# Seven block products for eight: a two-layer encoder trunk with Strassen's scheme in its large products

## The chip, the cores and the metric

One core of a Trainium2 chip runs the whole program. The metric is the device time of one execution in microseconds (us), as the median of several executions; lower is better. The core has TensorE (PE in the profile, its weight loads PEld), VectorE (DVE), ScalarE (ACT), GpSimd (POOL) and SyncE (SP, which issues all DMAs here). TensorE writes to PSUM, 8 banks of 128 partitions x 2 KB; everything else lies in SBUF.

## What is computed

x is 1024 tokens x 1024 features, float32. Layer A is multi-scale retention, layer B latent attention; both add to the residual stream.

```python
h = rmsnorm(x, g_pre)
proj = h @ w_in                           # q, k: 8 heads x 128; v, gate: 8 heads x 256
q, k, v, gate = jnp.split(proj, [...], axis=-1)
q = rope(q); k = rope(k) * 128 ** -0.5
# chunks of 64: inner scores, and a state R carried over chunks with a decay per head
o = groupnorm(inner + cross)
h1 = x + rmsnorm((jax.nn.silu(gate) * o) @ w_out, g_post)
# layer B
c_kv, k_r = split(rmsnorm(h1, g_kv) @ w_kv_a, [256])     # 256 + 64 columns
c_q, gate = split(rmsnorm(h1, g_pre) @ w_in_b, [384])    # 384 + 1024 columns
# queries, keys and values from the normalised latents, chunk-causal softmax attention, 8 heads
out = h1 + rmsnorm((jax.nn.silu(gate) * o) @ w_out_b, g_post)
```

The change touches four products: x with `w_in` (1024 x 1024 x 6144), the output product of layer A (1024 x 2048 x 1024), the latents (1024 x 1024 x 704) and layer B's gates (1024 x 1024 x 1024).

## The kernel before

A float32 operand of a large product is held as hi + lo, both of a rounded float32 type (fp32r): hi is the rounded value and lo the exact rest. `mm3` (lines 75 to 80) makes a product of three passes, lo x hi, hi x lo, hi x hi, into one PSUM bank. `split` (L84, L85) writes hi on ACT and lo on DVE; `split_scaled` (L89, L90) does the same with a factor for each partition.

**Memory.** `Heap` holds 51 blocks of 4 KB in every partition and hands them out in the order in which they were freed. A new tile in a block waits until the last reader of the old one is done.

**Order of the work.** The code is written in one order; the framework's planner then places each engine's instructions at build time, by that order among those that its own model holds to be ready. So passes of neighbouring k tiles can change places, and ready work can move into a gap. On the chip each engine keeps the order so fixed. `later(n, fn)` and `tick` write the mixing of a head n units of products behind its projections. `inv_rms` (L98 to L103: DVE, then a power on POOL) is emitted at high priority. All DMAs are issued by SP.

**Weights.** `weight_order` lists all weights in the order of use. `fetch` (L152) loads one of 128 x 1024, `prefetch` splits it, and two or three further ones are under way.

**Layer A** runs once for each half of 512 tokens. `load_x` brings x transposed, scales it by the gains and splits it (L254, L255). The products take this x before its normalisation; 1 / rms of the rows is computed on the side (`load_rows`, `ropeq_for`) and enters with the rotation tables (`csq`), the scale of v, and the gates (`rsb`, L369). `ret_pair` makes two heads: q and k with features on partitions (`features`, eight k tiles of three passes, 512 wide), then `rotate` on DVE (L312 to L315); v with tokens on partitions, 512 columns for both heads; the gates. `ret_scores`, `ret_states` and `ret_mix` mix the tokens, in blocks of 128. `ret_out` multiplies with `w_out_a` in two column halves, four PSUM banks each, eight heads deep; since both halves of the tokens run through all this, all weights of layer A are loaded and split twice. After the second half, `post_a` and `norm_transpose` build hT, the normalised and transposed input of layer B, split.

**Layer B.** `latents` makes c_kv with the rotary key (320 columns) and c_q (384 columns) for eight token tiles, in two groups of four, straight from PSUM into the norms. `gates` makes eight heads of gates, two halves each. The last four token tiles of layer A are normalised while the first group's latents run. `attention` follows, and is not touched by the change.

Of the kernel before, what the change touches and what calls it, by code (L numbers as in the profile page):

```python
# [10 lines left out]
F32 = mybir.dt.float32  # L11
# [14 lines left out]
NH = 8  # L26
# [3 lines left out]
LAG = 2  # L30


class Heap:
    """4 KB blocks of every partition, reused in the order in which they were freed."""
# [17 lines left out]

class Trunk:
# [12 lines left out]
    # ---------------------------------------------------------------- helpers  # L66
# [8 lines left out]
    def mm3(self, ps, lhs, rhs, first, last):  # L75
        """ps += lhs^T rhs with lhs = (hi, lo), rhs = (hi, lo)."""
        mm = self.nc.tensor.matmul
        mm(ps, lhs[1], rhs[0], start=first, stop=False)  # L78
        mm(ps, lhs[0], rhs[1], start=False, stop=False)  # L79
        mm(ps, lhs[0], rhs[0], start=False, stop=last)  # L80

    def split(self, hi, lo, src):
        """hi + lo = src."""
        self.nc.scalar.activation(hi, src, AF.Copy)  # L84
        self.nc.vector.tensor_sub(lo, src, hi.bitcast(F32))  # L85

    def split_scaled(self, hi, lo, src, scale):
        """hi + lo = src * scale, scale one number per partition."""
# [4 lines left out]
    def inv_rms(self, ss, n, tag, width):  # L93
        """(ss / n + eps) ** -0.5 for the columns of ss."""
# [3 lines left out]
    def _inv_rms(self, ss, n, tag, width):  # L98
        nc = self.nc
        r = self.small([P, width], tag, bufs=2)  # L100
        nc.vector.tensor_scalar(out=r, in0=ss, scalar1=1.0 / n, scalar2=EPS, op0=ALU.mult, op1=ALU.add)
# [6 lines left out]
    def tick(self):  # L108
        """One unit of a product is emitted: what has waited long enough follows it."""
# [7 lines left out]
    # ---------------------------------------------------------------- weights  # L117
    def weight_order(self):
        """All weights in the order of their use: (source, columns, gains)."""
        I, G = self.I, self.gains  # L120
        for half in range(2):
            for p in range(NH // 2):
                for j in range(12):
                    yield I["w_in_a"][p, j], (1024,), None
            for n in range(2):
                for k in range(NH):
                    yield I["w_out_a"][n, k], (1024,), None
# [918 lines left out]
```

## Time and profile before

| | |
|---|---|
| median of 3 runs | 1349.33 us (1348.61 to 1349.94) |
| profiled execution: its span | 1346.5 us, 2.8 us below the median of the runs |
| PE busy | 1329.0 us, 6952 matmuls |
| DVE, ACT, POOL busy | 829.2, 562.4, 72.1 us |
| DMA | 120.19 MB, 89 GB/s in the mean |
| mean granted TensorE clock | 0.999 |

The profile gives no other time of the profiled execution than its span; the 2.8 us are the difference to the other runs. "Busy" counts an engine from the start to the end of its instructions, where those of PE overlap. The chain of waits is followed back from the last instruction: at each step it goes to what released the instruction, or to the one before it on its engine. A row of a group has its line, engine, operation, output and inputs, count, then busy time and the mean of one instruction in ns, then the idle time of the engine ahead of it.

### The profile page before, as it was taken

The numbers are of one execution on the slowest core, as the hardware profiler recorded it, in microseconds if no ns is written. First come the engines' busy times: TensorE is split into PE (matmuls) and PEld (weight loads), VectorE is DVE, ScalarE is ACT, GpSimd is POOL, SyncE is SP. The second block draws the span as 40 slices with busy tenths as digits, with TensorE's granted clock in tenths as the row PEclk, the third lists the DMA queues.
The fourth block names the chain that finished last, engine by engine and source line by source line (L and its number), as shares of the span: only waits on it lengthen the run. The fifth ranks groups of instructions, "written<-read, shape, count | busy, mean of one in ns | idle before, by whom it ended". The sixth has DMA issues, their size and how long they took to land.

```text
span 1346.5 us, 17839 instructions
## 1 busy us (share of the span) xinstructions
PE 1329.0 (99%) x6952; PEld 1141.9 (85%) x6952; DVE 829.2 (62%) x1576; ACT 562.4 (42%) x998; POOL 72.1 (5%) x112
## 2 busy tenths in 40 slices
PE   7999999999999999999999999999999999999997
PEld 6888888888888888888888889988888989898886
DVE  4865666655747575656755865440089888888632
ACT  5533333335624333333435826431154545456311
POOL 0001000000001000000000102100000000000000
PEclk9999999999999999999999999999999999999999
DMA  9222232225445322232234351120011010122231
GB/s 357 87 79 73 63 99 74 79 83 182 132 156 182 95 78 63 63 110 78 64 110 122 116 177 63 48 73 30 24 32 42 25 42 25 42 73 79 88 116 47
DMA packets 38804, 120.19 MB, mean 89 GB/s; under 512 B 5184, under 2 KB 5440, under 8 KB 38720
## 3 DMA queue, kind: packets, MB, share of 16 engines
q1 hardware_dynamic: 38720, 119.06, 27.5%
q8 instruction: 54, 0.88, 0.3%
q14 instruction: 30, 0.25, 0.1%
HBM read 106.46 MB, written 8.39 MB: 85 GB/s over the span
## 4 chain that ended last, share of the span: by engine, by line
PE 94%; DVE 2%; ACT 1%; DMA 1%; issue 1%; SPq 1%; POOL 0%; DVEq 0%; POOLq 0%; ACTq 0%
PE acc L79 24%; PE acc L78 24%; PE acc L80 24%; PE r L78 4%; PE r L80 4%; PE r L79 4%; PE r L884 2%; PE S L838 1%; PE r L389 1%; PE r L478 1%; PE S L842 1%; PE S L839 1%; PE S L840 1%; PE S L843 1%; SPq L759 1%
## 5 line engine op out<-in xcount | busy, mean ns | idle before, releaser
L85 DVE TENSOR_TENSOR wlo<-wraw,whi 128x1024 fp32r<-128x1024 f32 (+4 forms) x165 | 192.4, 1173 | 141.1 <-ACT whi L84 123.6
L84 ACT ACTIVATE whi<-wraw 128x1024 fp32r<-128x1024 f32 (+4 forms) x165 | 167.6, 1022 | 169.6 <-PE acc L80 49.1
L78 PE MATMUL acc<-xhi,wlo 128*128 128x512 f32 x512 | 202.0, 395 | 6.5 <-ACT xhi L89 6.5
L79 PE MATMUL acc<-xlo,whi 128*128 128x512 f32 x512 | 200.8, 392 | 0.3 <-DVE xlo L90 0.3
L80 PE MATMUL acc<-xhi,whi 128*128 128x512 f32 x512 | 200.4, 391 | 0.0
L78 PEld LDWEIGHTS acc<-xhi,wlo 128*128 128x128 f32 x512 | 96.8, 189 | 25.3 <-ACT xhi L89 6.8
L80 PEld LDWEIGHTS acc<-xhi,whi 128*128 128x128 f32 x512 | 96.7, 189 | 20.2
L79 PEld LDWEIGHTS acc<-xlo,whi 128*128 128x128 f32 x512 | 96.8, 189 | 19.6 <-DVE xlo L90 1.3
L78 PE MATMUL acc<-whi,xlo 128*128 128x512 f32 x248 | 97.2, 392 | 0.0
L79 PE MATMUL acc<-wlo,xhi 128*128 128x512 f32 x248 | 96.6, 390 | 0.0
L80 PE MATMUL acc<-whi,xhi 128*128 128x512 f32 x248 | 96.4, 389 | 0.0
L854 ACT ACTIVATE p<-S,nm 128x896 f32<-128x896 f32 (+3 forms) x64 | 47.4, 741 | 54.9 <-DVE nm L851 50.2
L84 ACT ACTIVATE pT<-r 128x512 fp32r<-128x512 f32 (+2 forms) x96 | 44.5, 488 | 37.4 <-PE r L884 37.2
L460 ACT ACTIVATE y<-r,nb,rg 128x256 f32<-128x256 f32 x64 | 32.7, 562 | 54.5 <-DVE nb L457 54.5
L80 PEld LDWEIGHTS acc<-whi,xhi 128*128 128x128 f32 x248 | 46.6, 188 | 9.8
L78 PEld LDWEIGHTS acc<-whi,xlo 128*128 128x128 f32 x248 | 46.6, 188 | 9.3
L79 PEld LDWEIGHTS acc<-wlo,xhi 128*128 128x128 f32 x248 | 46.6, 188 | 9.1
L85 DVE TENSOR_TENSOR pT<-r,pT 128x512 fp32r<-128x512 f32 (+2 forms) x96 | 50.9, 549 | 4.9 <-ACT pT L84 4.5
L369 DVE TENSOR_TENSOR sg<-acc,rsb 128x512 f32<-128x512 f32 x32 | 22.1, 690 | 50.0 <-PE acc L80 50.0
L78 PE MATMUL acc<-whi,ylo 128*128 128x512 f32 x128 | 50.7, 396 | 0.0
L78 PE MATMUL acc<-whi,u 128*128 128x512 f32 x128 | 50.0, 391 | 0.0
L80 PE MATMUL acc<-whi,yhi 128*128 128x512 f32 x128 | 49.9, 390 | 0.0
(245 smaller groups left out, 3152.4 us busy)
## 6 DMA issues: line engine op xcount, KB each, us to landing
wraw<-in_w_in_a_dram SPq DMA_DIRECT2D x94, 512.0 KB, 3.7
wraw<-in_w_out_a_dram SPq DMA_DIRECT2D x32, 512.0 KB, 3.7
xr<-in_xT_dram SPq DMA_DIRECT2D x16, 256.0 KB, 4.2
xt<-in_x_dram SPq DMA_DIRECT2D x8, 512.0 KB, 6.0
xres<-in_x_dram SPq DMA_DIRECT2D x8, 512.0 KB, 4.5
h<-xres SPq DMA_DIRECT2D x8, 512.0 KB, 2.9
wraw<-in_w_gate_dram SPq DMA_DIRECT2D x8, 512.0 KB, 3.4
rr<-ra SPq DMA_DIRECT2D x64, 64.0 KB, 2.0
```

Source lines behind the costliest of these rows:

```text
L78: mm(ps, lhs[1], rhs[0], start=first, stop=False)
L79: mm(ps, lhs[0], rhs[1], start=False, stop=False)
L80: mm(ps, lhs[0], rhs[0], start=False, stop=last)
L84: self.nc.scalar.activation(hi, src, AF.Copy)
L85: self.nc.vector.tensor_sub(lo, src, hi.bitcast(F32))
L369: nc.vector.tensor_mul(c, ps, self.rsb[:, :HALF])
L389: nc.tensor.matmul(pa[:, c], k32[:, c], q32[:, c], start=True, stop=True)
L460: nc.scalar.activation(y[:, i * 256:(i + 1) * 256], po[:, i, :], AF.Identity, bias=nb[:, i:i + 1], scale=rg[:, i:i + 1])
L478: nc.tensor.transpose(pt[:, n * P:(n + 1) * P], y[:, n * 256 + e * P:n * 256 + (e + 1) * P], self.ident)
L759: nc.sync.dma_start(r[64 * part + 32 * x:64 * part + 32 * x + 32, :], a[64 * x + 32 * i:64 * x + 32 * i + 32, :])
L854: nc.scalar.activation(p[:, :w].rearrange("p (a b) -> p a b", a=pieces), view, AF.Exp, bias=nm, accum_out=sm)
L884: nc.tensor.transpose(pt[:, k, :], p[:, (k0 + k) * P:(k0 + k + 1) * P], self.ident)
```

## The change

The four products are cut into 2 x 2 blocks each and made by seven block products in place of eight, in Winograd's form of Strassen's scheme. With A the activations and B the weights: S1 = A21 + A22, S2 = S1 - A11, S3 = A11 - A21, S4 = A12 - S2, and T1 = B12 - B11, T2 = B22 - T1, T3 = B22 - B12, T4 = B21 - T2. A11 x B11 gives a, which is copied out of PSUM into U (ACT); S2 x T2 is added to U, and so on (DVE); A12 x B21, A22 x T4 and S4 x B22 go on accumulating in banks that already hold a, S3 x T3 and S1 x T1.

- **Layer A's input.** Both token halves together. x is normalised before its split (`scale_x`: squares on ACT, column sums with a matrix of ones on PE, `inv_rms`, a broadcast by PE, eight scalings on DVE). The seven left operands, 28 blocks, stay in SBUF for all 24 weight pairs. Until the second half of x is there, the first three pairs do the two products that need only the first half (`EARLY`).
- **Weights.** `Units` loads a weight pair once (two blocks), makes its four T sums on POOL (`make_sums`) and splits seven units of 128 x 512 columns, up to three ahead.
- **v** comes out with features on partitions like all others; `ret_values` transposes it back on PE (16 transposes of 128 x 128 a head). Rotation (`rotate_a`) takes its swapped halves by two ACT copies and works on both q and k at once on DVE. The scale of v and the factor of the gates are gone.
- **y** of each head and half goes to DRAM; `out_a` reads it back and works by 28 steps of 24 matmuls. Its S sums are on DVE, its T sums on POOL.
- **Layer B's operands** are built from both token halves in `post_a`. `latents` takes 704 columns as 2 x 352, weights scaled by their gains on POOL, results kept in SBUF (`lat`) ahead of the norms. `gates` uses `Units` and `pair`; six finished gates go to DRAM and come back.
- The unit order, heap and attention code stay. The DMA scratch is set to 1024 bytes.

The core of the diff:

```diff
+class Units:
+    def fetch(self):
...
+        for j in range(2):
+            r = self.raw[p][j]
+            T.nc.sync.dma_start(r, src[j])
...
+    def make_sums(self, p):
+        sub = T.nc.gpsimd.tensor_sub
+        sub(ta[:, lo], r0[:, hi], r0[:, lo])
+        sub(tb[:, lo], r1[:, hi], ta[:, lo])
+        sub(ta[:, hi], r1[:, hi], r0[:, hi])
+        sub(tb[:, hi], r1[:, lo], tb[:, lo])
...
+    def prep(self):
+        u = T.heap.get("unit", F32R)
+        T.split(u[:, :HALF], u[:, HALF:], src)
...
+WINOGRAD = ("B11", "T2", "T3", "T1", "B21", "T4", "B22")
+    def product(self, ps, units, name, more=False):
+        u = units.next()
+        for k in range(4):
+            c, x = slice(k * P, (k + 1) * P), slice((k % 2) * HALF, (k % 2 + 1) * HALF)
+            self.mm3(ps, (u[:, :HALF][:, c], u[:, HALF:][:, c]), [b[:, x] for b in self.X[name][k // 2]],
+                     not more and k == 0, k == 3, more)
...
+    def pair(self, units, sink, steps="abcdefg", st=None):
+            if s == "a":
+                st["a"] = self.bank("acc")
+                self.product(st["a"], units, "A11")
+                st["u"] = self.small([P, HALF], "u2", bufs=4)
+                self.nc.scalar.copy(st["u"], st["a"])
+            elif s == "b":
+                b = self.bank("acc")
+                self.product(b, units, "S2")
+                add(st["u"], b, st["u"])
+            elif s == "c":
+                self.product(st["c"], units, "S3")
+                add(st["u3"], st["c"], st["u"])
+            elif s == "d":
+                self.product(st["d"], units, "S1")
+                sink(1, 1, st["d"], st["u3"])
+            elif s == "e":
+                self.product(st["a"], units, "A12", more=True)
+                sink(0, 0, st["a"], None)
+            elif s == "f":
+                self.product(st["c"], units, "A22", more=True)
+                sink(1, 0, st["c"], st["u"])
+            elif s == "g":
+                self.product(st["d"], units, "S4", more=True)
+                sink(0, 1, st["d"], st["u"])
...
     def layer_a(self):
+        x = self.load_x(0)
+        units.fetch()
+        self.scale_x(x)
+        A["A11"], A["A12"] = x[:2], x[2:]
+        self.left_sums(A, ("A11", "A12"))
...
+        x = self.load_x(1)
+        for sink, st in early:
+            self.pair(units, sink, "ae", st)
+        self.scale_x(x)
+        A["A21"], A["A22"] = x[:2], x[2:]
+        self.left_sums(A, ("A22", "S1", "S2", "S3", "S4"))
+        for sink, st in early:
+            self.pair(units, sink, "bcdfg", st)
+        for p in range(EARLY, 3 * NH):
+            self.pair(units, make(p))
...
+    def out_a(self):
+            if prod == 6:
+                return [left(1, 0, b), left(1, 1, b), left(0, 0, b)], [right(0, 0, b), right(0, 1, b), right(1, 1, b)]
...
+        run(1, X)
+        run(2, X, True)
+        run(6, Y)
+        run(7, X)
+        run(5, Y)
+        run(4, X, True)
+        for t in range(HT):
+            add(y[HT + t][:, n0], X[t], U[t])
+            self.post_a(HT + t, y[HT + t], gpost)
+        run(3, Y, True)
+        self.left_sums(self.A, ("A22",))
+        self.left_sums_keep(self.A)
+        for t in range(HT):
+            add(y[t][:, n1], Y[t], U[t])
+            self.post_a(t, y[t], gpost)
...
     def latents(self):
+        run(X, "S1", "T1")
+        run(X, "A22", "T4")
+        self.left_sums(self.A, ("A11", "A12", "S2", "S3", "S4"))
+        run(X, "A11", "B11")
+        run(Y, "S2", "T2")
+        run(X, "A12", "B21", True)
+        run(X, "S3", "T3")
+        self.latent_tiles(1, lat[HT:], rk)
+        run(X, "S4", "B22")
+        self.latent_tiles(0, lat[:HT], rk)
...
     def gates(self):
+        for p in range(NH // 2):
+            self.pair(units, sink(p))
+        for h in range(away):
+            self.gT[h] = heap.get("gT")
+            nc.sync.dma_start(self.gT[h], self.gd[h])
```

More of the change, by code (lines that the diff above doesn't have):

```diff
@@ L30 @@
 LAG = 2
+LAT = 704
+LH = LAT // 2
 class Heap:
@@ L188, in run @@
         self.h1 = dp.tile([NT, P, DM], F32, name="h1")
+        self.yd = [[dp.tile([P, DM], F32, name=f"yd{h}_{half}") for half in range(2)] for h in range(NH)]
+        self.gd = [dp.tile([P, DM], F32, name=f"gd{h}") for h in range(NH)]
         self.ident = self.small([P, P], "ident")
```

910 lines of the change are left out of this document (536 added, 374 removed).

## The prediction

> **What bounds the kernel now.** I read the engine totals first, then the chain that ended last, then what TensorE waited for, then the stages.
>
> ```profile
> PE 1329.0 (99%) x6952; PEld 1141.9 (85%) x6952; DVE 829.2 (62%) x1576; ACT 562.4 (42%) x998; POOL 72.1 (5%) x112
> ...
> PE 94%; DVE 2%; ACT 1%; DMA 1%; issue 1%; SPq 1%; POOL 0%; DVEq 0%; POOLq 0%; ACTq 0%
> ```
>
> TensorE (PE) is busy for 1329.0 of 1346.5 us and makes up 94% of the chain. The view of TensorE's waits:
>
> ```profile
> PE acc L78 <- ACT xhi L89: 6.5, 1, 6.5
> PE r L564 <- DVE hT L85: 1.2, 1, 1.2
> ```
>
> Its only long wait is the start. So the time is the number of matmuls times their spacing, plus some 17 us of gaps. By stage (columns: stretch, its length, busy time of PE, PEld, DVE, ACT, POOL, granted clock, DMA share, GB/s):
>
> ```profile
> 0.00:30.00 30.00, 23.23 (x91) 18.24 (x92) 14.62 (x20) 19.04 (x27) 1.72 (x7) 1.00 0.93 353
> ...
> 45.00:345.00 300.00, 300.00 (x1517) 253.73 (x1516) 190.58 (x324) 116.88 (x170) 21.10 (x32) 1.00 0.29 92
> ```
>
> In the retention stage (second row) PE has no gap at all, DVE has a third free and POOL is nearly idle. A change that lowers the count of matmuls gains their whole spacing there, as long as the operands still come in time.
>
> **What a matmul costs.** A matmul's listed duration overlaps the next one, so I take starts from the chain of waits (start, us, what):
>
> ```profile
> 178.03 0.23 PE acc L78
> ...
> 187.56 0.23 PE acc L78
> 188.02 0.23 PE acc L80
> 188.25 0.87 PE r L478 x8
> ...
> 839.12 0.17 PE acc L78
> ...
> 841.20 0.17 PE acc L78
> ```
>
> From 178.03 to 187.56 lie 14 steps of three 512-wide matmuls: 0.227 us each. From 839.12 to 841.20 lie 4 steps of three 384-wide ones: 0.173 us each. Eight 128-wide transposes take 0.87, 0.109 each.
>
> ```profile
> L78 PE MATMUL acc<-whi,hT 128*128 128x384 f32 x64 | 21.8, 340 | 0.0
> L78 PE MATMUL acc<-whi,hT 128*128 128x320 f32 x64 | 20.0, 313 | 0.0
> ```
>
> A 320-wide one lasts 27 ns less than a 384-wide one, so its spacing is about 0.147, and a 352-wide one lies between, 0.160.
>
> **What is removed.** Seven block products replace eight. Counted from the loops, with three passes each:
> - Layer A's projections: 2304 matmuls become 24 x 84 = 2016. 288 x 0.227 = -65.4 us.
> - Its output product: 768 become 28 x 24 = 672. -21.8 us.
> - Gates: 384 become 336. -10.9 us.
> - Latents: 192 of 320 and 192 of 384 columns (61.4 us) become 336 of 352 (53.8 us). -7.6 us.
>
> Added on TensorE: v now leaves its product transposed, and 16 transposes for each of 8 heads turn it back: 128 x 0.109 = +13.9 us. The sums of squares by TensorE (one column) fall in a gap at the start. Net **-91.8 us** on the bounding engine.
>
> **The start.** Now the first matmul waits for one 128 KB piece of weights and one of x (timeline):
>
> ```profile
> 6.52 0.79 PE L78 MATMUL acc<-xhi,wlo 128*128 128x512 f32 x1 [6.52 <-ACT xhi L89]
> ...
> 16.77 1.06 ACT L278 ACTIVATE xt<-xt 128x1024 f32<-128x1024 f32 x1 [0.22 <-DMA xt<-in_x_dram]
> ...
> 21.80 0.17 DVE L101 TENSOR_SCALAR rs<-ss 128x4 f32<-128x4 f32 x1 [3.99 <-ACT xt L278]
> ...
> 22.05 1.03 POOL L102 TENSOR_TENSOR rs<-rs,mhalf 128x4 f32<-128x4 f32 x1 [20.76 <-DVE rs L101]
> ...
> 24.34 2.50 DVE L85 TENSOR_TENSOR wlo<-wraw,whi 128x1024 fp32r<-128x1024 f32 x2 [2.37 <-ACT whi L84]
> ```
>
> Since x is now normalised before its split, nothing can start until the half's x (2 MB, eight DMAs) is there: at 353 GB/s about 6 us, so near 9 us. Then come the last square (1.06 on ACT), a sum (0.7), the sums of squares and the power (about 2.5), the broadcast, eight scalings of 0.75 on DVE (6 us) and the splits. The first matmul comes near 18 us, and full flow near 22, when DVE has the first lo. In 0 to 30 us before, 91 matmuls x 0.227 = 20.6, so 9.4 us were lost; now some 20. **+10** (bounds 6 and 18). The six early products, the cover for the second half, are 72 x 0.227 = 16.3 us and end near 37. The second half's x has landed by then (5 MB through 353 GB/s), but on DVE stand eight scalings (6 us) and then A22's lo, S1's two sums, S1's lo, S2's differences, S2's lo, at 2.5 us a pair by the last row above. Product "b" of S2 is next in PE's order, "c" (S3) and "g" (S4) behind it; "d" of S1 can go first. S1 is split some 7 us after the scalings. **+9** (bounds 2 and 20).
>
> **Retention.** PE per head (both halves) goes from 78.3 us (next fence: a pair of heads, one half, is the same work) to 78.3 - 36 x 0.227 + 1.7 = 71.9. DVE must stay below that. The stretch, and the groups of DVE in it:
>
> ```profile
> 82.54:160.84 78.30, 78.30 (x396) 66.08 (x395) 49.04 (x83) 28.91 (x41) 5.63 (x8) 1.00 0.25 74
> ```
>
> ```profile
> L85 DVE TENSOR_TENSOR wlo<-wraw,whi 128x1024 fp32r<-128x1024 f32 x13 | 15.8, 1218 | 7.7 <-ACT whi L84 7.6
> ...
> L90 DVE SCALAR_TENSOR_TENSOR v<-acc,rs,v 128x512 fp32r<-128x512 f32 x4 | 3.0, 745 | 3.2 <-ACT v L89 3.2
> L313 DVE TENSOR_TENSOR tmp<-acc,csq 64x512 f32<-64x512 f32 x4 | 2.8, 693 | 0.1
> L312 DVE TENSOR_TENSOR qk<-acc,csq 128x512 f32<-128x512 f32 x4 | 2.8, 690 | 1.9 <-PE acc L80 1.9
> L369 DVE TENSOR_TENSOR sg<-acc,rsb 128x512 f32<-128x512 f32 x4 | 2.8, 689 | 9.7 <-PE acc L80 9.7
> L314 DVE TENSOR_TENSOR tmp<-acc,csq 64x512 f32<-64x512 f32 x4 | 2.7, 684 | 0.1
> L315 DVE TENSOR_TENSOR qk<-qk,tmp 128x512 f32<-128x512 f32 x4 | 2.7, 681 | 0.0
> ...
> L85 DVE TENSOR_TENSOR q<-qk,q 128x512 fp32r<-128x512 f32 x2 | 1.4, 688 | 0.8 <-ACT q L84 0.8
> ```
>
> Gone are the weights' lo (15.8), the rotation (11.0), v (3.0) and sg (2.8): 16.4 stays. New: 21 unit splits at 0.69 (14.5), 15 additions to U at 0.69 (10.3), six 1024-wide rotation steps at 1.22 (7.3), four lo of v (2.8). Total 51 of 71.9 us. ACT (28.9 of 78.3 now) stays further off. So neither bounds by its sum.
>
> New on POOL are the T sums, four 128x512 subtractions per unit pair. No row shows one. The nearest are a group of POOL, and three pieces of the timeline:
>
> ```profile
> masks.py:199 POOL TENSOR_SCALAR_AFFINE_SELECT ident<-ident 128x128 f32<-128x128 f32 x1 | 0.3, 295 | 0.1
> ```
>
> ```profile
> 815.14 1.29 DVE L544 SCALAR_TENSOR_TENSOR xres<-y,ro,xres 128x1024 f32<-128x1024 f32 x1
> ...
> 814.57 0.54 POOL L102 TENSOR_TENSOR ro<-ro,mhalf 128x1 f32<-128x1 f32 x1 [59.19 <-DVE s L540]
> 815.29 1.53 POOL L102 TENSOR_TENSOR ro<-ro,mhalf 128x1 f32<-128x1 f32 x1 [0.19 <-DVE ro L101]
> ```
>
> Below: DVE's 0.69 for the same shape. Above: POOL's 128-wide select at 0.295, times four for the width, times two for the second input, 2.36. I take twice DVE's, 1.4, or 17 us per head. The last three rows show a hazard: the same one-column power takes 0.54 us alone and 1.53 while DVE reads two SBUF operands. If the exclusion also works the other way, DVE's 51 and POOL's 17 add up to 68 of 71.9, still below the bound but with little slack for an order that the planner fixed beforehand. **+5** (0 to 62, the latter with 2.36: 51 + 28 = 79.6 against 71.9, for 8 heads).
>
> The Trainium skill has both halves of this. "GPSIMD Engine Reference" (Performance versus the Vector engine) gives 4497 ns for a 2048-wide two-input add against 2293 on VectorE, so an estimate of 1.1 to 1.2 us here; by that the retention sum would be 51 + 14 = 65. "SBUF — State Buffer" (Who interferes with whom) says that a VectorE instruction with two SBUF inputs contends with a GpSimd instruction that reads SBUF; the 1.53 us row agrees.
>
> **Output product of layer A.** 28 steps of 24 x 0.227 = 5.45 us. Product 6 loads six blocks a step (3.1 MB; at 353 GB/s 8.9 us) and makes t1, t2 on POOL and s1, s2 and two lo (4 x 1.22) on DVE. Covered if the loads run ahead during products 1 and 2 (43.6 us, 15 MB by that rate against 8.4 of their own); without that cover 4 x 3.5 = 14 us. **+6** (0 to 25).
>
> **Into the latents.** After the last product, four tiles must pass norms, transposes and evictions before A11 is whole; before the change the same tail ran under group 0's latents (chain, then ACT's timeline):
>
> ```profile
> 812.27 0.70 ACT junk L529 x2
> ...
> 831.26 1.23 PE r L564 x8
> ```
>
> ```profile
> 816.46 1.06 ACT L557 ACTIVATE hn<-xres 128x1024 f32<-128x1024 f32 x1 [1.32 <-DVE xres L544]
> ...
> 819.24 1.14 ACT L559 ACTIVATE hn<-xres,rh 128x1024 f32<-128x1024 f32 x1
> ```
>
> That is 19 us to the last transposes, and PE waited 1.2 of it. Now ACT has about 5 us a tile (two squares, a scaling at 1.06 to 1.15, four copies), so A11 is split some 27 us after the product. The cover is two products of 48 x 0.160 = 7.7 us and 32 transposes (3.5): 19 us. Behind A11's product stand S2, A12, S3, S4. The weights' gains (16 POOL multiplications) and T sums must be there as well. **+10** (2 to 30).
>
> **The rest.** Latents to gates: block space is full (28 of 51 blocks hold X), so the first units come late: **+4** (0 to 10). Gates to attention: the first attention weights queue on SP behind six gate reloads and two tables, 4 MB or 11 us, partly before the end: **+4** (0 to 10). Restarts:
>
> ```profile
> 8.79 0.43 PE acc L78
> ...
> 11.65 0.43 PE acc L78
> ```
>
> After the idle start the matmuls came every 0.43 us until 12 us, a loss of 2.3 us. Three new gaps may each repeat that: **+3** (0 to 7).
>
> **Sum.** In the profiled execution: 1346.5 - 91.8 + 10 + 9 + 5 + 6 + 10 + 4 + 4 + 3 = 1305.7; the median of the runs lies 2.8 us above its span: **1309 us**. The low ends give 1268, all high ends over 1430.
>
> **Rivals.**
> 1. *The covers hold.* The planner places ready work into gaps (the trace shows passes out of the code's order), and only the start and half of the rest remain: 10 + 5 + 12 = 27 us in place of 51: 1285. For it: before, PE had 17 us of gaps in all. Against: 28 fixed blocks of X leave little room to run ahead. 0.29.
> 2. *The stage boundaries are exposed.* Start 30, output 14, latents 22, others 20, total 86: 1344 or a little less. For it: the long chain of DVE operations at the start has no cover. 0.16.
> 3. *VectorE and GpSimd exclude each other* (slower). Where: unit splits and rotations against the T sums in retention. It binds from (71.9 - 51.3) / 12 = 1.7 us a subtraction and eats the gain from about 1.7 + 40 / 96 = 2.1. At 2.36: +62 in retention less the 5, and some 15 in the other stages: 1380. For it: 1.53 against 0.54. Against: only part of DVE's work has two SBUF inputs. 0.11.
> 4. *No change*: gaps that happen to equal 92 us. 0.03.
>
> My forecast has 0.41; its own range is 1295 to 1330. The range **1276 to 1350** holds rivals 1 and 2 and leaves out the lowest ends and rival 3. 0.2% is 2.7 us, about what runs of this kernel can tell from none: faster 0.85, same 0.03, slower 0.12.
>
> **What would show it.** PE's busy count must fall by 288 + 96 + 48 + 48 matmuls and gain 128 transposes. Right: waits of PE on the split of X near 18 and 37 to 46 us, no wait longer than 1 us in retention, some 10 us before A11's first product. Wrong: PE waiting on unit splits all through retention (rival 3), or a spacing other than 0.227, or a first product before 12 us.

## The result, and the profile after

The changed kernel takes **1445.21 us** (median of four runs, 1445.04 to 1448.13) against 1349.11 (1348.61 to 1349.94) for the kernel before on the same chip: a ratio of 1.0715, 95% interval 1.07 to 1.0731. It is slower; I had predicted 1309. The profiled execution took 1445.18 with a span of 1443.4. In what follows a single run is told from another only where they differ by more than some 6 us: repeated runs of one kernel below differed by up to 5.8.

Engine totals and the chain that ended last, after:

```profile
PE 1295.5 (90%) x6664; PEld 1102.4 (76%) x6664; DVE 994.2 (69%) x1721; ACT 638.2 (44%) x1173; POOL 330.1 (23%) x296
...
PE 40%; POOL 6%; DVE 5%; ACT 3%; issue 2%; DMA 2%; SPq 0%; POOLq 0%; DVEq 0%; ACTq 0%
```

The count of TensorE fell as it should: 6952 - 480 products + 128 transposes + 64 short ones for the sums of squares = 6664. But TensorE is 90% busy, not 99%. The chain of after breaks off: its shares add up to 58% of the span, 40 of them TensorE's, so its 40% can't be set against the 94% of before. TensorE's waits (total, times, longest):

```profile
PE acc L825 <- ACT hn L819: 33.1, 4, 22.5
PE acc L174 <- ACT xhi L180: 16.0, 2, 13.4
PE r L531 <- DVE qk L479: 11.7, 8, 3.5
PE acc L174 <- DVE unit L181: 11.0, 2, 6.6
...
PE r L174 <- DVE R L595: 6.8, 6, 1.1
```

No single wait makes 97 us. By stage, first after (start to 100 us; rest of layer A; output product; its tail; latents; gates; attention), then before (layer A's halves with their output products second and fourth; latents; gates; attention; ahead of the first row lies the start, 6.52 us without TensorE). First number behind the stretch: its length; second: busy time of TensorE.

```profile
0.00:100.00 100.00, 62.51 (x248) 50.54 (x248) 64.59 (x84) 42.90 (x54) 20.60 (x20) 0.86 0.26 97
100.00:672.00 572.00, 542.88 (x2778) 454.53 (x2778) 406.66 (x695) 251.01 (x443) 162.49 (x144) 0.99 0.19 63
672.00:830.00 158.00, 146.50 (x655) 120.45 (x655) 116.67 (x113) 64.61 (x77) 58.83 (x29) 0.99 0.52 184
830.00:888.00 58.00, 28.56 (x128) 24.39 (x129) 35.20 (x36) 33.30 (x65) 40.11 (x32) 0.69 0.32 116
888.00:971.00 83.00, 64.60 (x357) 61.28 (x356) 45.56 (x69) 38.98 (x78) 18.59 (x41) 0.85 0.04 13
971.00:1069.00 98.00, 84.64 (x365) 69.51 (x366) 51.94 (x73) 42.00 (x76) 24.98 (x24) 0.92 0.34 124
1069.00:1443.40 374.40, 365.79 (x2136) 321.68 (x2135) 273.55 (x656) 165.43 (x385) 4.52 (x8) 0.99 0.17 55
```

```profile
6.52:318.40 311.88, 311.62 (x1543) 261.95 (x1544) 195.38 (x323) 125.03 (x180) 18.31 (x29) 1.00 0.33 110
318.40:411.60 93.20, 93.20 (x437) 77.96 (x436) 56.67 (x73) 47.40 (x66) 4.72 (x5) 1.00 0.50 161
411.60:718.30 306.70, 306.70 (x1537) 259.59 (x1535) 188.99 (x320) 109.96 (x163) 22.18 (x32) 1.00 0.31 95
718.30:814.10 95.80, 95.80 (x460) 80.22 (x459) 64.39 (x92) 53.05 (x84) 5.99 (x8) 1.00 0.38 124
814.10:884.60 70.50, 69.34 (x454) 68.78 (x453) 34.72 (x97) 39.30 (x91) 15.26 (x23) 1.00 0.17 61
884.60:973.90 89.30, 88.61 (x398) 73.18 (x396) 13.53 (x14) 17.88 (x28) 0.54 (x1) 1.00 0.13 40
973.90:1346.50 372.60, 363.69 (x2136) 320.22 (x2136) 274.21 (x657) 166.47 (x386) 4.43 (x8) 1.00 0.18 55
```

Length less busy time is TensorE's idle time. Summed over the rows it is 17.5 us before and 147.9 after. The two right-hand columns of the table are from the same view of two runs told below.

| stage | before: length, idle | after | e1 (sums on VectorE) | e15 (repaired) |
|---|---|---|---|---|
| layer A but its output | 625.1, 6.8 | 672.0, 66.6 | 638.5, 45.8 | 634.4, 37.4 |
| output product and tail | 189.0, 0 | 216.0, 40.9 | 214.1, 39.2 | 186.6, 16.9 |
| latents | 70.5, 1.2 | 83.0, 18.4 | 82.3, 18.5 | 90.3, 24.3 |
| gates | 89.3, 0.7 | 98.0, 13.4 | 88.7, 7.2 | 83.9, 1.5 |
| attention | 372.6, 8.9 | 374.4, 8.6 | 374.6, 9.0 | 374.0, 10.0 |

Busy time flatters, because a matmul at half clock is busy twice as long. From start to start of neighbouring matmuls in the whole trace, less the spacing at full speed for their width, the 96.9 us divide so: work -88.0; gaps over 0.3 us +144.2 (5.6 to 149.8); spacing of about twice the normal +27.1 (4.8 to 31.9); small delays +13.6 (1.2 to 14.8).

### The profile page after: what moved, and what is told of

Read it like the earlier page. It is cut to its first block, busy times and chain, and to the rows that moved or that the text cites. A ratio compares the mean times of both kernels' runs of the same rounds, so it can differ in the third digit from the quotient of the medians.

```text
span 1443.4 us, 17924 instructions
## 1 busy us (share of the span) xinstructions
PE 1295.5 (90%) x6664; PEld 1102.4 (76%) x6664; DVE 994.2 (69%) x1721; ACT 638.2 (44%) x1173; POOL 330.1 (23%) x296
## 4 chain that ended last, share of the span: by engine, by line
PE 40%; POOL 6%; DVE 5%; ACT 3%; issue 2%; DMA 2%; SPq 0%; POOLq 0%; DVEq 0%; ACTq 0%
PE acc L174 9%; PE acc L175 9%; PE acc L176 9%; PE r L1204 2%; POOL t L692 1%; PE S L1158 1%; DMA wl<-in_w_out_a_dram 1%; PE S L1162 1%; PE S L1163 1%; PE S L1160 1%; PE S L1159 1%; PE r L174 1%; POOL wt L855 1%; POOL wl L850 1%; PE r L176 1%
## 5 line engine op out<-in xcount | busy, mean ns | idle before, releaser
L174 PE MATMUL acc<-xhi,unit 128*128 128x512 f32 x784 | 316.0, 403 | 37.3 <-ACT xhi L180 16.0
L175 PE MATMUL acc<-xlo,unit 128*128 128x512 f32 x784 | 311.9, 398 | 4.7 <-DVE xlo L181 4.7
L176 PE MATMUL acc<-xhi,unit 128*128 128x512 f32 x784 | 310.1, 396 | 0.0
L174 PEld LDWEIGHTS acc<-xhi,unit 128*128 128x128 f32 x784 | 150.9, 192 | 71.4 <-ACT xhi L180 16.5
L175 PEld LDWEIGHTS acc<-xlo,unit 128*128 128x128 f32 x784 | 150.9, 193 | 34.7 <-DVE xlo L181 5.7
L176 PEld LDWEIGHTS acc<-xhi,unit 128*128 128x128 f32 x784 | 150.6, 192 | 31.8
L180 ACT ACTIVATE unit<-wsum 128x512 fp32r<-128x512 f32 x112 | 68.8, 629 | 125.5 <-POOL wsum L100 56.8
L181 DVE TENSOR_TENSOR unit<-wsum,unit 128x512 fp32r<-128x512 f32 x112 | 87.3, 791 | 38.7 <-ACT unit L180 38.5
L181 DVE TENSOR_TENSOR unit<-wraw,unit 128x512 fp32r<-128x512 f32 x84 | 67.9, 809 | 2.6 <-ACT unit L180 2.6
L180 ACT ACTIVATE unit<-wraw 128x512 fp32r<-128x512 f32 x84 | 52.8, 630 | 37.5 <-PE acc L176 21.4
L180 ACT ACTIVATE pT<-r 128x512 fp32r<-128x512 f32 (+2 forms) x96 | 44.5, 488 | 36.6 <-PE r L1204 36.5
L174 PE MATMUL acc<-thi,slo 128*128 128x512 f32 x128 | 50.5, 398 | 5.8 <-ACT u L765 3.3
L181 DVE TENSOR_TENSOR pT<-r,pT 128x512 fp32r<-128x512 f32 (+2 forms) x96 | 50.9, 549 | 4.9 <-ACT pT L180 4.6
L175 PE MATMUL acc<-tlo,shi 128*128 128x512 f32 x128 | 50.7, 396 | 1.7 <-DVE tlo L181 1.7
L176 PE MATMUL acc<-thi,shi 128*128 128x512 f32 x128 | 50.6, 395 | 0.0
L174 PE MATMUL acc<-whi,u 128*128 128x512 f32 x128 | 50.1, 391 | 0.0
```

Source lines behind the costliest of these rows:

```text
L174: mm(ps, lhs[1], rhs[0], start=first, stop=False, skip_group_check=more)
L175: mm(ps, lhs[0], rhs[1], start=False, stop=False, skip_group_check=more)
L176: mm(ps, lhs[0], rhs[0], start=False, stop=last, skip_group_check=more)
```

## The experiments

Each run below is one execution beside the kernel before (1347.8 to 1349.3), unless more are named.

**GpSimd's T sums.** First the sums to VectorE, then no sums at all.

```diff
-        sub = T.nc.gpsimd.tensor_sub
+        sub = T.nc.vector.tensor_sub
```

> The T sums of layer A's and the gates' units (four 128x512 subtractions per pair of products) go from GpSimd to VectorE; nothing else changes. Theory P (GpSimd and VectorE hold each other up: in the trace of the changed kernel the units' lo take 771 and 860 ns instead of 688 and the rotation's sum 1468 instead of about 1290 when they meet a subtraction, and TensorE waits 36 us in gaps between 99 and 672 us): VectorE gets 8.3 us a head more of plain work but loses the stretch of some 5 us; the period of a head falls from 76.5 to 73 to 74 us, and the time from 1445 to about 1420. Theory L (TensorE's order is fixed and VectorE's rotations and states come late in it, whoever makes the sums): the extra 8.3 us a head on VectorE makes them later still; 1445 to 1465.

```diff
-        if what[0] == "T" and p not in self.sums:
-            self.make_sums(p)
...
-        src = (self.raw[p][int(name[1])] if name[0] == "r" else self.sums[p][name == "tb"])[:, c]
+        src = self.raw[p][int(name[1]) if name[0] == "r" else int(name == "tb")][:, c]
```

> The T sums of layer A's and the gates' units are left out: the units T1 to T4 take the raw halves of their blocks, so the numbers are not the reference's; TensorE's work, the splits and the loads stay. GpSimd keeps only the norms' powers there. Theory P: the gaps of retention go almost all, 30 to 40 us, and the first T units at 77 to 99 us come some 10 us earlier: 1395 to 1415. Theory L: the waits on rotations and states stay (3.8 us a head); only the units' lo get faster: 1435 to 1445.

Measured: **1399.99** and 1393.1. Theory L is out, and the gain is more than theory P had asked for: VectorE got more work (994.2 to 1019.4 us busy) and the kernel became 45 us faster. The sums on VectorE (75.8 us by their rows, some 677 ns each) cost only 7 us more than none at all. Groups by shape, after, then e1 (the lines are the same in both):

```profile
L181 DVE TENSOR_TENSOR unit<-wsum,unit 128x512 fp32r<-128x512 f32 x112 | 87.3, 791 | 38.7 <-ACT unit L180 38.5
L181 DVE TENSOR_TENSOR unit<-wraw,unit 128x512 fp32r<-128x512 f32 x84 | 67.9, 809 | 2.6 <-ACT unit L180 2.6
```

```profile
L181 DVE TENSOR_TENSOR unit<-wsum,unit 128x512 fp32r<-128x512 f32 x112 | 73.6, 682 | 5.1 <-ACT unit L180 5.0
L181 DVE TENSOR_TENSOR unit<-wraw,unit 128x512 fp32r<-128x512 f32 x84 | 56.8, 682 | 3.5 <-ACT unit L180 3.5
```

Both are operations with two SBUF inputs. One meeting in the timeline of after, and the spread of two groups (ns: least/median/most):

```profile
395.97 1.22 DVE L478 TENSOR_TENSOR xs<-xs,sin 128x1024 f32<-128x1024 f32 x1
396.07 2.27 POOL L97 TENSOR_TENSOR wsum<-wraw 128x512 f32<-128x512 f32 x1 [13.05 <-DVE qk L479]
397.10 0.68 DVE L353 TENSOR_TENSOR u<-acc,u 128x512 f32<-128x512 f32 x1
397.70 1.72 DVE L479 TENSOR_TENSOR qk<-qk,xs 128x1024 f32<-128x1024 f32 x1
398.29 2.26 POOL L99 TENSOR_TENSOR wsum<-wraw,wraw 128x512 f32<-128x512 f32 x1
399.34 1.75 DVE L181 TENSOR_TENSOR unit<-wraw,unit 128x512 fp32r<-128x512 f32 x1
399.48 0.66 PE L531 MATMUL r<-ident,qk 128*128 128x128 f32 x4 [0.54 <-DVE qk L479]
```

```profile
L97 POOL TENSOR_TENSOR wsum<-wraw x28: 1276/1297/2272, 12.0 to 1032.1; 128x512 f32<-128x512 f32 x28
...
L181 DVE TENSOR_TENSOR unit<-wraw,unit x84: 657/682/1779, 15.4 to 1043.6; 128x512 fp32r<-128x512 f32 x84
```

The subtraction that starts at 396.07 beside a VectorE operation takes 2.27, not 1.30; the rotation that starts beside it takes 1.72, not 1.22; the next unit's low half 1.75, not 0.68. The addition from PSUM between them keeps its 0.68. TensorE waits 0.54 us for that rotation (last row). The Trainium skill, "SBUF — State Buffer" (Who interferes with whom), says that GpSimd shares a pair of SBUF ports with VectorE and that this pair is an exclusive lock; the trace agrees, since the second of two such instructions ends about its own length behind the first: the rotation ends at 399.42, 1.1 us behind the first subtraction (398.34), and the low half at 401.09, 0.5 us behind the second (400.55), nearly their own lengths.

The collision is not the only path from these sums to TensorE. The third head in after, then the split of q in the same head of e1:

```profile
249.74 1.15 ACT L180 ACTIVATE unit<-wsum 128x512 fp32r<-128x512 f32 x2 [9.39 <-POOL wsum L100]
250.79 0.61 ACT L180 ACTIVATE q<-qk 128x512 fp32r<-128x512 f32 x1
251.44 0.69 DVE L181 TENSOR_TENSOR q<-qk,q 128x512 fp32r<-128x512 f32 x1 [3.67 <-ACT q L180]
255.11 0.68 DVE L447 TENSOR_TENSOR vt<-acc,u 128x512 f32<-128x512 f32 x1
255.85 0.50 PE L174 MATMUL acc<-xhi,unit 128*128 128x512 f32 x1 [0.79 <-DVE vt L447]
```

```profile
232.66 0.63 ACT L180 ACTIVATE q<-qk 128x512 fp32r<-128x512 f32 x1 [4.68 <-DVE qk L479]
```

In after the split of q stands in ScalarE's queue behind two splits of T units, and these wait until GpSimd has ended its fourth sum at 249.70. The rotation of q was done at 245.50; its split begins 5.3 us later, and VectorE's work behind it is late down to the sum of v that TensorE waits for. In e1 the split begins 0.04 us behind the rotation. TensorE's waits in six heads (176 to 636 us) are 6.8 us for the state R, 5.4 for the rotation, 3.9 for the sum of v and 2.2 for v's low half; in e1 (165 to 600) 3.9 for R, 1.6 for the rotation and none for v. So e1 and e2 show what it costs that GpSimd makes the sums. How much of it is the collision, which also stretched these four sums from some 5 us to 7.5, and how much the queues behind late sums, no run separates.

What the place of the sums is worth in retention, by the same rotation in both kernels:

```profile
L479 DVE TENSOR_TENSOR qk<-qk,xs x16: 1207/1220/2307, 98.1 to 630.0; 128x1024 f32<-128x1024 f32 x16
```

```profile
L479 DVE TENSOR_TENSOR qk<-qk,xs x16: 1211/1215/1218, 90.2 to 596.0; 128x1024 f32<-128x1024 f32 x16
```

From the first rotation of the first head to the last of the last lie 531.9 us after and 505.8 in e1: 26.1 us over seven heads, 3.7 a head. The start gave 7.9 (98.1 to 90.2) and the gates 9.3 (table): 43 of the 45 us. In the gates the four sums of the first pair are not held up (1.26 to 1.30 us each, at 962.14 and from 972.31 to 977.09). By the trace it is queues there: the powers of the latents' norms stand between these sums on GpSimd, and the T units' splits stand on ScalarE behind a norm that waits for such a power, until 980.93.

**The start.** The second half's normalisation behind the first early pair; then normalisation left out; then two orders of the start on top of e7 (below).

```diff
-        EARLY = 3
+        EARLY, MID = 3, 0
...
-        for sink, st in early:
+        for n, (sink, st) in enumerate(early):
             self.pair(units, sink, "ae", st)
-        self.scale_x(x)
+            if n == MID:
+                self.scale_x(x)
```

> The sums of squares, power and scalings of the second half of x are written behind the first of the three early pairs, not behind all three. Theory S (serial chain: TensorE's sums of squares for the second half stand behind all early products, so VectorE starts its 28 us of scalings, differences and splits at 50.9 us): that chain starts about 10 us earlier, the wait ahead of the first S2 or S3 product (13.6 us) goes to about 4: 1433 to 1437. Rival B (blocks: the first T sums find blocks only when x's are freed, GpSimd begins at 76.6 us): the wait only moves from x to the T units, 1442 to 1446. It may also cost: the first early products share TensorE with the transposed sums.

```diff
-        self.scale_x(x)
...
-        self.scale_x(x)
```

> The normalisation of x is left out (sums of squares, power, broadcast and the eight scalings of both halves), so the numbers are not the reference's; the splits, differences and products of layer A stay. It prices the step that the words of the change name. Theory S (the normalisation stands serially ahead of both halves): the first product comes at 12 to 13 us and not at 21.7, and the S operands 12 to 15 us earlier: 1420 to 1430. Rival D (VectorE's differences and splits of the five S operands, 22 us, and the blocks for the T sums are what the second half waits for): only the first half's part is gained: 1436 to 1441.

Measured: 1435.81 and **1420.74**. Theory S in both: 9 us for the place, 24 us for the whole step. In e6 the first product started at 15.5 us, not 21.7, and the output product at 647.2, not 672.0: all of it was gained before. After's chain on VectorE and what TensorE did meanwhile:

```profile
44.88 0.83 DVE L199 TENSOR_SCALAR rs<-r 128x1 f32<-128x1 f32 x4 [9.17 <-PE r L431]
50.91 5.36 DVE L440 SCALAR_TENSOR_TENSOR xr<-xr,gains,r 128x512 f32<-128x512 f32 x8 [5.19 <-PE r L436]
56.18 1.22 DVE L181 TENSOR_TENSOR xlo<-xr,xhi 128x1024 fp32r<-128x1024 f32 x1
...
74.95 2.35 DVE L181 TENSOR_TENSOR xlo<-s,xhi 128x1024 fp32r<-128x1024 f32 x2
...
64.28 0.80 PE L174 MATMUL acc<-xhi,unit 128*128 128x512 f32 x1 [13.41 <-ACT xhi L180]
```

VectorE stood idle for 9.17 us for sums of squares that stood behind the early products in TensorE's queue, and then had 26 us of work in a row (50.9 to 77.3) that the products need.

```diff
-        self.left_sums(A, ("A11", "A12"))
+        for j, name in enumerate(("A11", "A11", "A12", "A12")):
+            self.scale_blocks(x, [j])
+            self.operand_block(name, x[j])
...
-        self.left_sums(A, ("A22", "S1", "S2", "S3", "S4"))
+        self.scale_blocks(x, [2, 3])
+        self.left_sums(A, ("A22",))
+        self.scale_blocks(x, [0, 1])
+        self.left_sums(A, ("S1", "S2", "S3", "S4"))
+        for sink, st in early:
+            st["f"] = self.bank("r")
+            self.product(st["f"], units, "A22")
```

> The run with four edits, and the start is reordered: each block of x is split right behind its own two scalings, the products of A22 (which needs no sum) come first in all three early pairs, in banks of their own, then S1's, and S3 and S4 are made block by block. The arithmetic is the same up to the order of sums. If VectorE's serial chain is what the start waits for, A22's three products (8.2 us) are new cover and the first product's second pass comes 3 us earlier: 1356 to 1361 from 1367.9. If the chain's end decides whatever stands ahead of it: 1364 to 1368.

```diff
-        self.left_sums(A, ("S1", "S2", "S3", "S4"))
         for sink, st in early:
             st["f"] = self.bank("r")
             self.product(st["f"], units, "A22")
+        self.left_sums(A, ("S1", "S2", "S3", "S4"))
```

> The run with the reordered start, and A22's three products are written ahead of the sums S1 to S4, so that the next units' low halves no longer stand on VectorE behind those sums (58 to 71 us in that run, where TensorE waited 12.7 us for a unit). If that queue was the wait: the 12.7 us fall to about 4 and the time from 1370.6 to 1360 to 1363. If the chain of sums decides anyhow: TensorE waits the same time for S1's, S2's or S3's low half, 1367 to 1371.

Measured: 1370.55 against e7's 1367.9, no gain; then 1365.49 (two runs, 1364.50 and 1366.49; ratio to before 1.012, 1.0091 to 1.015). In e13 TensorE waited 12.72 us in one piece for a unit's low half behind the sums in VectorE's queue; e17 mended that, and its longest wait there was

```profile
79.55 0.80 PE L174 MATMUL acc<-xhi,unit 128*128 128x512 f32 x1 [4.92 <-DVE unit L181]
```

and, for this stretch:

```profile
50.00:100.00 50.00, 41.28 (x171) 31.37 (x170) 48.16 (x58) 22.29 (x28) 0.00 (x0) 0.93 0.07 21
```

VectorE, the third busy time, works for 48.16 of 50 us, which leaves an order little to gain. That the amount of its work sets the start is argued from this and from e6; no run took away its sums and splits alone.

**Into the latents.** The latents' weights to VectorE, alone; the last output product turned so that its tiles end apart, alone.

```diff
-        gsub = nc.gpsimd.tensor_sub
+        gsub = nc.vector.tensor_sub
...
-                        nc.gpsimd.tensor_mul(v[:, :, a:b], v[:, :, a:b],
+                        nc.vector.tensor_mul(v[:, :, a:b], v[:, :, a:b],
```

> The 16 gain multiplications and 8 T sums of the latents' weights go from GpSimd to VectorE; nothing else changes. Theory Q (the powers of the last four tiles' norms stand in GpSimd's queue behind this weight work, 848 to 870 us): the 22.7 us gap ahead of the latents and the 4.4 and 7.7 us after it fall to about 10 together: 1420 to 1427. Rival T (the tail of norms, transposes and copies is 27 us against a cover of 19 anyway, as I had counted ahead): the gap only falls to some 12 to 15 us and VectorE's 16 us more of work push the splits: 1435 to 1442.

```diff
-        run(3, Y, True)
+        for b in range(4):
+            fill(0, 1)
+            units.append(ready.popleft())
+            fill(1, 1)
...
         for t in range(HT):
+            for b, (s2, t2) in enumerate(units):
+                for e in range(2):
+                    c = slice(e * HALF + t * P, e * HALF + (t + 1) * P)
+                    self.mm3(Y[t], [x[:, c] for x in s2], [x[:, e * HALF:(e + 1) * HALF] for x in t2],
+                             False, b == 3 and e == 1, True)
...
             add(y[t][:, n1], Y[t], U[t])
```

> Only the last block product of layer A's output (product 3) is turned: its four inner blocks are split first, and then each tile of 128 tokens takes its eight steps in a row, so the four tiles of the first token half are finished 5.45 us apart and not all at the end. Theory C (cover: the tail of norms, transposes and copies behind the last product, about 27 us for four tiles, has a cover of two latent products): three of four tails run under the product itself; the waits ahead of the latents, 33 us in all, fall by 20 to 25: 1420 to 1427. Theory Q (GpSimd's queue: the norms' powers stand behind 22 us of gains and T sums of the latents' weights): the tiles come earlier but their powers don't; 1436 to 1445.

Measured: 1437.82 and 1447.27. The first lies in the range of its rival T: it gained 7.4 us, and the longest wait on hn fell from 22.5 to 11.2. The second gave nothing. Counted from the start of the output product they are 11.0 and 3.3 us shorter than after; layer A, which neither edit touches, took 3.6 and 5.4 us longer in these executions. The queue of GpSimd in after, and TensorE's row there:

```profile
865.89 4.39 POOL L855 TENSOR_TENSOR wt<-wl,wt 128x704 f32<-128x704 f32 x2
870.24 1.05 POOL L200 TENSOR_TENSOR ro<-ro,mhalf 128x1 f32<-128x1 f32 x2
...
876.73 3.68 PE L825 MATMUL acc<-ident,hn 128*128 128x128 f32 x16 [22.50 <-ACT hn L819]
```

The powers come at 870.24, although VectorE had the first one's input ready at 862.3. In e5 TensorE waited for the weights' splits in place of the tiles: its row "acc L174 <- ACT thi L180" went from 1.3 to 11.8 us while the row of hn fell from 33.1 to 22.3.

Then the edits together: all T sums of the unit pairs, output product and latents on VectorE, e4's place, e5's turn (e7); the last latent product by tile too (e8). What these have beside the edits above:

```diff
-        add, sub, gsub = nc.vector.tensor_add, nc.vector.tensor_sub, nc.gpsimd.tensor_sub
+        add, sub, gsub = nc.vector.tensor_add, nc.vector.tensor_sub, nc.vector.tensor_sub
...
-        run(X, "S4", "B22")
         for t in range(HT):
+            for m in range(2):
+                for e in range(2):
+                    c = slice(e * HALF + t * P, e * HALF + (t + 1) * P)
+                    self.mm3(X[t][:, :LH], [x[:, c] for x in self.X["S4"][m]], [x[:, e * LH:(e + 1) * LH] for x in t2s[m]],
+                             m == 0 and e == 0, m == 1 and e == 1)
             add(lat[t][:, n1], X[t][:, :LH], U[t])
```

> All T sums of units, output product and latents and the latents' gains on VectorE, the second half's normalisation behind the first early pair, and the last output product by tile, together. If the single gains (45, 7.5, 9.5 and what the last product by tile gives) add up, 1445 less 45, 7.5, 9.5, 20 and some 5 for the output product's T sums: about 1358. If VectorE becomes the bound by the moved work (16 us at the latents, 1.2 us times 20 in the output product): 1370 to 1385.

> As the run before with four edits, and the last latent product by tile as well. The waits between latents and gates (4.7 us on the norms of the latents, 6.6 us on the first units) should fall by about 5: some 1353, if the cover is what lacks there; no change if the gates' first units are late for their own work.

Measured: **1367.9** and 1378.57. The output product up to its tail, 158.0 us with 11.5 idle after, takes 146.0 with 1.3 idle in e15 (which has these edits): 12 us, and t1 to t4 are what was taken off GpSimd there. The turn of product 3 is not the cause, since e16, without it, needs some 146.5. But ahead of the latents and in them 24 us of waits stayed; two of e7's rows:

```profile
PE acc L838 <- ACT hn L832: 16.4, 4, 10.2
...
PE r L174 <- ACT thi L180: 7.5, 1, 7.5
```

Why e8 lost 10.7 us against e7 was not followed up; by its trace the waits on hn grew from 16.4 to 21.9 us and the one on the weights' high half from 7.5 to 9.7. On top of e7: the latents' weights made ahead of product 4, with the splits of A22 and S1 behind the tiles (e9); e9 with later transposes of the latents and earlier attention weights (e10); e10 with the weights ahead of product 5 (e11); e7 without the norms of the first half's tiles (e12); e13 and the boundary edits (e14).

First the edit of e9, then that of e10 (in e14 and e15 too), then that of e12.

```diff
+        self.latent_weights()
         run(4, X, True)
...
-                        nc.vector.tensor_mul(v[:, :, a:b], v[:, :, a:b],
-                                             G[:, g + k0:g + k0 + 2, None].to_broadcast([P, 2, b - a]))
+                        for k in range(2):
+                            nc.scalar.activation(v[:, k, a:b], v[:, k, a:b], AF.Copy,
+                                                 scale=G[:, g + k0 + k:g + k0 + k + 1])
```

```diff
-        self.later(3, kv_tail)
-        self.later(5, cq_tail)
+        self.later(6, kv_tail)
+        self.later(9, cq_tail)
...
+        for _ in range(2):
+            self.fetch()
         for h in range(away):
             self.gT[h] = heap.get("gT")
```

```diff
+        if g < HT:
+            nc.sync.dma_start(self.h1[g], x)
+            nc.scalar.activation(hn, y, AF.Copy)
...
+            return
         s = self.small([P, 1], "s1", bufs=2)
         nc.scalar.activation(hn, y, AF.Square, accum_out=s)
```

> As the run with four edits, and: the gains of the latents' weights (on ScalarE now) and their T sums (on VectorE, one in place) are made ahead of product 4 of the output, 43 us before its end, and the splits of the half-1 operands A22 and S1 are written behind the last tile, so that they no longer stand ahead of the tiles' squares on ScalarE (793 us in that run). If the 10.4, 5.2, 3.5 and 7.6 us gaps ahead of the latents come from queues in which work of the latents stands ahead of the tiles' norms, they fall from 27 to about 10: 1350 to 1354. If they are the bare length of a tile's chain (square, power, gain, add, square, power, scaling, transposes, copies, some 12 us behind the last product, then the split): 1362 to 1368.

> As the run before, and the transposes of the latents wait for 6 and 9 products instead of 3 and 5, and the first two attention weights are loaded ahead of the six gate reloads. The waits on the norms of the latents (3.7, 1.6, 1.0, 0.9 and 1.1 us) and on the first attention weights (6.2 us) should go: 10 to 14 us below the run before. If the gates' first unit (4.5 us) and the chains of the tiles decide there: 3 to 6 us below it.

> As the run with all edits, but the latents' weights are made ahead of product 5 (22 us earlier still). If VectorE or ScalarE is too full between products 4 and 3 to take this work without delaying the tiles, a gain of 3 to 6 us against the run before; if it fits, the same within 2 us.

> The run with four edits, and for the four tiles of the first token half both norms, the gain and the residual sum are left out on the way from the output product to the transposes (the tile is only copied; the numbers are not the reference's). If the length of that chain is what TensorE waits for ahead of the latents (gaps of 10.4, 5.2 and 3.5 us in the run with four edits, 1367.9), some 16 us go: 1350 to 1354. If the latents' weights on VectorE (804 to 823 us) or the splits of the operands would be late anyway: 1360 to 1366.

> As the run before, and the splits of A22 and S1 of the latents behind the second tile, the latents' transposes 6 and 9 products late, and the first attention weights ahead of the gate reloads. If these boundaries are separate, their gains add: 8 to 12 us below the run before. If each hands its wait to the next boundary: 0 to 4 us below it.

Measured: 1372.95, 1370.21, 1370.22, 1361.26, 1369.26. None but e12, which leaves work out, differs from e7 by more than runs differ. In e12 TensorE's waits on hn fall from 16.4 us to 4.3. Of its row for the weights' high half 7.5 us stand in e7 too; the other 3.4, ahead of the first latent product, are new:

```profile
PE r L174 <- ACT thi L180: 10.9, 2, 7.5
```

Without the norms only 6.6 us go in all: part of the wait comes back on the splits. That VectorE and ScalarE have too much to do between the output product and the latents, in whatever order, is argued from e9 to e14, where no order gained; no run shows it alone.

**The repaired kernel**, four runs each (e15: e7 with e10's later transposes and earlier attention weights; e16: the same with product 3 whole):

> The run with four edits, and the latents' transposes wait for 6 and 9 products and the first two attention weights are loaded ahead of the gate reloads: the best that these edits are good for. If the covers at the last boundaries are separate from the rest: 1368 less 6 to 10, so 1358 to 1362, still slower than the kernel before by 0.7 to 1%. If the wait moves on to the gates' units or the first heads: 1364 to 1368.

> The same without the turned product 3 (its four tiles are finished together again). Alone it gave nothing (1447.3 against 1445). If it needed the free queues to help: 8 to 15 us slower than the run with it. If the tail's work on ScalarE and VectorE decides, not when the tiles come: the same within 4 us.

Measured: 1371.24 (1369.96 to 1371.86; ratio to before 1.0162, 1.0145 to 1.0179) and 1371.11 (1367.37 to 1373.18; 1.0159, 1.014 to 1.0178). Finishing the tiles apart is worth nothing, and the later transposes only moved the wait: TensorE's wait on the latents' norms, 4.7 us after, is 11.2 in e15.

```profile
PE r L943 <- ACT ckv L938: 11.2, 4, 6.0
```

So of the 96 us some 74 (e15) to 80 (e17) were had back, and no version beats the kernel before. e8, e9, e13 and e15 came out slower than both cases that had been set down for them: the repairs, too, were overrated.

## Why the prediction was wrong

**TensorE's work** was right: -91.8 predicted, -88.0 measured (the 64 short sums of squares, taken as nothing, are the difference). What failed are the losses set against it: 51 us predicted, 184.9 measured (144.2 + 27.1 + 13.6).

**Retention, "+5 (0 to 62)"**, is, with the start, the largest error: 26 us in seven heads by e1. The numbers it was made of held. A subtraction took 1.40 to 1.55 us on average (1.4 taken), and VectorE's work in a head of some 76 us was some 54 (406.66 of 572 us in the second row of the stages), 51 by the sum. In e1 a head takes some 72 us (505.8 over seven, a few us too many, since the two rotations of a head do not stand at one time), against 71.9 predicted. The step that failed is "*neither bounds by its sum*", and with it rival 3's condition, "*It binds from (71.9 - 51.3) / 12 = 1.7 us a subtraction*". The loss was there at 1.40 to 1.55 us, with VectorE over a quarter idle and GpSimd over two thirds: TensorE does not wait for an engine that is full, but for one rotation, state or sum of v that is late, because a link in its chain met a subtraction or stood in a queue behind a late sum. Rival 3 had named the first of these paths alone. The prediction expected "no wait longer than 1 us in retention"; there were three of 2.7 to 3.5 us on the rotation and six of 1.1 on the state.

**The start, "+10" and "+9".** Right in kind and place, too small: in the first 100 us 168 matmuls of 512 columns (38 us) and 80 short ones ran, so some 57 us were lost, against 9.4 before and 19 more predicted. The failed step is "*The second half's x has landed by then*": VectorE could not begin when x landed, but only when TensorE had come to the sums of squares behind all early products (e4: 9 us). The normalisation is 24 of these us by e6; the rest, as argued above, is VectorE's sums and splits, for which the sum had set only the 9 of the second half, and the T units that stand behind them in its queue.

**Output product, "+6 (0 to 25)"**: 12 us, by e15's 146.0 against 158.0. The step "*Covered if the loads run ahead*" asked for the loads and not for GpSimd's t1 to t4.

**Into the latents, "+10 (2 to 30)"**: 29.4 us idle in the tail, the upper end. I had named the weights' gains and sums ("*must be there as well*") and not asked in which queue they stand: ahead of the norms' powers. That queue is 7.4 us of the whole time by e3, 11.0 of the stretch from the output product on. The rest I put down to the tail's own work on ScalarE and VectorE, which I took as a length of 27 us against a cover of 19, while each part also delays the splits of the latents.

**Restarts, "+3 (0 to 7)"**: 27 us. I counted three gaps; by the starts in the trace 35 were longer than 1 us (one before), and after most of the long ones the matmuls come at half speed for a while (last section).

**The rivals and the form of the sum.** Rival 2 (boundaries exposed) had 86 us for what is 110 us of idle time outside retention and attention after, and rival 3 was right in part: both came about, and I had set them against each other, 1344 or 1380. In the sum, too, each boundary was priced with the others' cover intact. The runs show the waits in series on VectorE and ScalarE: mending one (e5, e13, e15) uncovers the next.

## What to carry to other kernels

When a change trades matmuls for elementwise work, ask not whether each helper engine stays below its total, but which of its results TensorE waits for and what stands ahead of them in that engine's queue. Do not move two-input SBUF work to GpSimd beside a VectorE that does the same kind on the path: here taking 12 subtractions a head, and the gates', back to VectorE gained 45 us, through collisions and queues together. A bounding engine that ran at 99% has no slack to lose; its gain must be larger than every boundary's tail, and its restarts, together.

## What was not expected of the hardware

A restart costs more than its gap. Behind the 22.50 us gap the 16 transposes at 876.73 take 3.68 us, 0.23 each in place of 0.109. A gap of 4.09 us follows, which ends at 884.50, and TensorE's rows are still slow (352 columns, starts):

```profile
888.86 0.49 PE L174 MATMUL r<-thi,xlo 128*128 128x352 f32 x1
889.15 0.41 PE L175 MATMUL r<-tlo,xhi 128*128 128x352 f32 x1
889.39 0.32 PE L176 MATMUL r<-thi,xhi 128*128 128x352 f32 x1
889.56 0.32 PE L174 MATMUL r<-thi,xlo 128*128 128x352 f32 x1
```

They come every 0.29 us until 889.15, some 4.7 us behind the second restart, and soon every 0.16; the granted clock is 0.50 from 876.7 to 889.3 and 1.00 from there to 895. In all this is 27 us more than before, 1.9% of the span. The Trainium skill, "TensorE: Matmul & The Clock Gate" (What's actually happening), gives half clock after an idle window of about 3.4 us and full clock after as long a busy one, and puts the ramp under 1% of a typical kernel span. The trace agrees in kind, but in this kernel with its many gaps the ramp costs the 1.9%, and the length of a gap alone does not tell what follows it: behind the 1.14 us gap that ends at 367.00 the granted clock is 0.51 until 370.4, behind the 3.27 us gap that ends at 703.45 it is 1.00.
